# Attention inside a hybrid encoder: query pairs turned in a projection bank, two fillers moved, the keys' banks reordered, and the gates' running maxima turned at the seventh head

## The chip, the cores and the metric

One core of a Trainium2 chip runs the whole program. Its engines are TensorE (PE, with PEld for the weight loads that overlap it), VectorE (DVE), ScalarE (ACT), GpSimd (POOL) and SyncE (SP), which here issues nearly all DMA transfers. Each engine works through its own list of instructions in order; semaphores let it wait for the others. The metric is the time of one execution on the device in microseconds (us), given as the median of several executions.

## The reference

The program is one layer of a bidirectional encoder on two inputs of 512 tokens by 1024 channels: a half-step SwiGLU network, a mixing block, a second half-step SwiGLU network and a last normalisation. The change touches the mixing block alone:

```python
h = rms_norm(x, mix_norm)
proj = h @ w_in                      # queries, keys, values, memory q/k/v, 16 gate columns, output gates
aq = apply_rope(rms_norm(aq, q_norm), cos, sin)      # 8 query heads of 64
ak = apply_rope(rms_norm(ak, k_norm), cos, sin)      # 2 key/value heads
att = gqa_block_attention(aq, ak, av)                # softmax(q k / 8) v over all 512 tokens
mem = mlstm_bidirectional(mq, mk, mv, gate_pre, mlstm_gate_bias, o_pre, mlstm_head_norm)
merged = sigmoid(g_att) * (att @ w_up_att) + sigmoid(g_mlstm) * (mem @ w_up_mlstm)
x = x + merged @ w_out
```

The memory (`mlstm`) runs over the tokens in both directions with four heads. It needs, per direction and head, cumulative sums of the logarithms of the forget gates and running maxima over the tokens, so that its exponentials stay bounded. In the kernel these come from the 16 gate columns.

## The kernel before, in words

All matrix products are in float32 accuracy: each operand is split into a rounded high part and the remainder, and a product is made of three matmuls of the parts. So a result that is to be multiplied again goes through a split, one ACT instruction (L715, the high part) and one DVE instruction (L716, the remainder).

The mixing block, `mix`, is run twice, first for `s=0`, about 640 to 983 us, then for `s=1`, about 983 to 1403 us. In each pass:

- `tok_proj` (matmuls at L800) projects the keys, the values and the 16 gate columns for the four blocks of 128 tokens into four PSUM banks, and then the queries. The banks come from pools: `mm` (three banks, `MM`), `pss` (two, `PS`), `pst` (two, `PT`) and `pso` (one, `PO`).
- `gates` turns the gate columns into logarithms, sums them up with six small float32 products (L970), and makes running maxima along the tokens in a tile of 32 rows (L980 and L981). It sends the rows to DRAM (`ebuf`, L979). `gate_tops` later transposes the running maximum and the total maximum back (L988 and L989), and a DVE copy (L990) puts them into `st`. `mem_scales` (L1070 to L1081) derives the memory's scales from that with a dozen small DVE steps.
- `mem_rows` loads a head's row from `ebuf` into all partitions (L1061) and adds a mask to it (L1064). Its results lie in slots 0 to 3 of an eight-slot tile called `box`: head 0 takes slot 0 for the loaded row of the first direction, slot 1 for its masked copy, and slots 2 and 3 for the second direction.
- Attention goes head by head and, within a head, by four blocks. `score(h, b)` (L1091) makes the scores of 128 queries against 512 keys in a `pss` bank; DVE takes the row maximum (L1094), ACT the exponential with its sum (L1096), DVE the reciprocal (L1097), and ACT (L1099) or DVE (L1101) the scaling. `turn_keys(Ps, kb)` transposes the four query blocks' probabilities for one block of keys into a `pst` bank (L1107) and splits the result (L715 and L716). `values` multiplies it with the values into `pso` (L1118).
- Before heads 2, 4 and 6, `q_turn` transposes two query heads with four small matmuls (`pair_turn`, L900) and evacuates them with ACT and DVE (L1041 and L1042).
- Between these steps stand fillers: single matmuls of independent gate projections (L820, 512 columns each) that `among(n)` places n at a time. Their results are taken by ACT and DVE (L864 and L865) from an `mm` bank.

Attention's matmuls and the fillers are kept on PE in the order in which the code calls them. All other instructions, and the whole lists of ACT, DVE and SP, are ordered by a scheduler that runs when the kernel is built. The loop is:

Of the kernel before, what the change touches and what calls it, by code (L numbers as in the profile page):

```python
# [16 lines left out]
P = 128  # L17
# [9 lines left out]
def encoder(ctx, tc, I, outs):  # L27
    nc = tc.nc
# [13 lines left out]
    def nm(s):  # L42
        n_id[0] += 1
        return f"{s}_{n_id[0]}"
# [8 lines left out]
    boxes = {}  # L53
# [6 lines left out]
    def T2(dtype=F32, tag="t2"):  # L60
        if tag in ("eb", "ac"):
            i = boxes[tag]
            boxes[tag] += 1
            return boxes["tile"][:, i % 4 + (4 if tag == "ac" else 0), :]
        if tag == "R":
            return spool.tile([P, S], dtype, tag="R", bufs=2, name=nm("R"))
        n = {"t2": 11, "f2": 4}[tag]
        return tpool.tile([P, S], dtype, tag=tag, bufs=n, name=nm(tag))
# [47 lines left out]
    def PT():  # L116
        return pt.tile([P, S], F32, tag="t", name=nm("pst"))

    def f(ap):
        return ap.bitcast(F32)  # L120
# [7 lines left out]
    ones = cpool.tile([P, P], F32, name="ones")  # L128
# [157 lines left out]
    def load_w(view, key, park=True):  # L286


        if key in parked:
            d, shape = parked[key]  # L290
            w2 = wpool.tile(shape, F32R, tag="w8", bufs=4, name=nm("w"))
            for i in range(2):
                nc.sync.dma_start(f(w2[:, i]), d[:, i])
            return w2[:, 0], w2[:, 1]
        raw = fetch_w(view)
        with shifted(-WEIGHTS):
            hi, lo = split_w(raw, V_)
        if not park:
            return hi, lo
        shape = [P, 2] + list(raw.shape[1:])  # L300
        parked[key] = d, _ = dpool.tile(shape, F32, name=nm("wpark")), shape
        for i, t in enumerate((hi, lo)):
            nc.sync.dma_start(d[:, i], f(t))
        return hi, lo
# [424 lines left out]
    tabs = []  # L729
# [41 lines left out]
    def go(*units):  # L771
        for load, comp in units:
            held.append((comp, load()))
            while len(held) > ahead[0]:
                c, w = held.pop(0)
                c(w)
# [6 lines left out]
    def tok_proj(xh, xl, cols, kk, done, banks):  # L783

        N = sum(n for _, n in cols)
        p = []

        def load(k0):
            return load_w([win_v[:, k0:k0 + kk, c:c + n] for c, n in cols], ("in", cols[0], k0))

        def comp(k0, w):
            wh, wl = w
            if not p:
                p.extend(b() for b in banks)
            for kl in range(kk):
                k = k0 + kl
                for b in range(4):
                    bs = slice(b * P, (b + 1) * P)
                    for i, (a, w_) in enumerate(((xh, wh), (xh, wl), (xl, wh))):
                        nc.tensor.matmul(p[b][:, :N], a[:, k, bs], w_[:, kl, :],  # L800
                                         start=(k == 0 and i == 0), stop=(k == KD - 1 and i == 2))
            if k0 + kk == KD:
                done(p)

        return [(lambda k0=k0: load(k0), lambda w, k0=k0: comp(k0, w)) for k0 in range(0, KD, kk)]
# [29 lines left out]

    OUT = 3
    FILLER = 5,3
    FIRST = 9

    def mix(s, xh, xl, early=None, extra=None, after=None):  # L840

# [8 lines left out]
        def F2(dtype=F32):  # L850
            return T2(dtype, "f2")
# [42 lines left out]
            yield tt(v, v, cg.unsqueeze(2).to_broadcast([P, 4, 2, DA]), op=ALU.mult)  # L894
            yield tt(v, v, m, op=ALU.add)

        def pair_turn(o, keep):
            p = PT()
            for b in range(4):
                keep(nc.tensor.transpose(p[:, b * P:(b + 1) * P], o[:, b, :], ident))  # L900
            return p
# [17 lines left out]
        qraw, rq = mg[:, 4:8, :], []  # L919
# [18 lines left out]
        def gs(tag):  # L938
            t = small(32, tag)
            return t, t.rearrange("p (d b h) -> p d b h", d=2, b=4)  # L940
# [7 lines left out]
        def gates():  # L948
            Gb = Gt.rearrange("p (b c) -> p b c", b=4)
            V_.tensor_tensor(Gb, Gb, gbias.unsqueeze(1).to_broadcast([P, 4, 16]), op=ALU.add)  # L950
            Gv = Gt.rearrange("p (b d g h) -> p b d g h", b=4, d=2, g=2)

            Fs, Fv = gs("Fs")
            Is, Iv = gs("Is")
            for dst, g in ((Fv, 1), (Iv, 0)):
                G_.tensor_copy(dst[:, 0], Gv[:, :, 0, g, :])
                for b in range(4):
                    G_.tensor_copy(dst[:, 1, 3 - b], Gv[:, b, 1, g, :])
            fa, _ = gs("fa")
            V_.scalar_tensor_tensor(fa, Fs, -1.0, Fs, op0=ALU.mult, op1=ALU.min)  # L960
            nc.scalar.activation(fa, fa, AF.Exp)
            nc.scalar.activation(fa, fa, AF.Ln, bias=1.0)
            nc.scalar.activation(warm, fa[:, 0:1], AF.Exp)
            Lt, _ = gs("Lt")
            V_.scalar_tensor_tensor(Lt, Fs, 0.0, fa, op0=ALU.min, op1=ALU.subtract)
            p = PT()
            for d in range(2):
                rhs = Lt[:, d * 16:(d + 1) * 16]
                for j, lhs in enumerate((tabs[2][:, 2 * d, :], tabs[2][:, 2 * d + 1, :], ones)):
                    nc.tensor.matmul(p[:, j * 32 + d * 16:j * 32 + (d + 1) * 16], lhs, rhs, start=True, stop=True)  # L970
            V_.tensor_copy(cs, p[:, 0:96])
            et, ev = gs("fa")
            V_.tensor_tensor(et, Is, cs[:, 32:64], op=ALU.add)
            p = PT()
            nc.tensor.transpose(p[0:32, 0:P], et, ident)
            rows = F2()[0:32]
            er, run = rows[:, 0:P], rows[:, P:2 * P]
            V_.tensor_copy(er, p[0:32, 0:P])
            nc.sync.dma_start(ebuf.rearrange("d b h s -> (d b h) s"), er)  # L979
            V_.tensor_tensor_scan(run[:, ::-1], er[:, ::-1], er[:, ::-1], NEG, op0=ALU.max, op1=ALU.max)  # L980
            V_.tensor_tensor_scan(run[0:16], er[0:16], er[0:16], NEG, op0=ALU.max, op1=ALU.max)  # L981
            top = rows[:, 2 * P:2 * P + 1]
            V_.tensor_reduce(top, er, axis=AX.X, op=ALU.max)
            return run, top
# [50 lines left out]
        def q_rope(pr):  # L1035
            return rope_steps(qraw[:, :, pr * P:(pr + 1) * P], rq[0][:, :, 2 * pr:2 * pr + 2], tabs[0])

        def q_turn(pr, keep):
            p = pair_turn(qraw[:, :, pr * P:(pr + 1) * P], keep)
            for h, own, other in ((2 * pr, lower, upper), (2 * pr + 1, upper, lower)):  # L1040
                nc.scalar.activation(qT[own, h, :], p[own, :], AF.Copy)  # L1041
                V_.tensor_tensor(qT[other, h, :], p[own, :], f(qT[own, h, :]), op=ALU.subtract)  # L1042

        go(*tok_proj(xh, xl, [(512, 256), (2304, 16)], 2, kv_done, (PS, PS, MM, MM)))
        if early:
            early()
        go(*tok_proj(xh, xl, [(0, 512)], 2, q_done, (MM, PO, MM, MM)), mem_qk(0, 0), mem_qk(0, 1))
# [88 lines left out]
        def among(n):  # L1136
            for _ in range(n):
                if not between:
                    if not held:
                        return  # L1140
                    c, w = held.pop(0)
                    if queue:
                        load, c2 = queue.pop(0)
                        held.append((c2, load()))
                    between.extend(c.steps(w))
                between.pop(0)()
# [6 lines left out]
        for b in range(4):  # L1153
            Ps.append(score(0, b))
            next(rope, None)
            among(FIRST)
        last = None
        for h in range(HA):
            nxt = []
            for b in range(4):  # L1160
                if h in (0, 2, 4) and b == 2:
                    q_turn(h // 2 + 1, pin)
                if (h, b) == (0, 1):
                    gate_tops(*tops)
                if (h, b) in ((0, 3), (2, 3)):
                    rope = q_rope(h // 2 + 2)
                if h < 4:
                    next(rope, None)
                if h + 1 < HA:
                    nxt.append(score(h + 1, b))  # L1170
                among(FILLER[0])
                pp = turn_keys(Ps, b)
                among(FILLER[1])
                if last:
                    values(*last)
                last = h, b, pp
                if extra and b == 2 and h in (2, 3, 4):
                    extra[h - 2]()
            Ps = nxt
# [320 lines left out]
    def keep(k, eng=None):  # L1500
        pin(keep_x(0, k, banks[k], x0r[k], eng))
# [156 lines left out]
    def mid_parts(s):  # L1658
# [10 lines left out]
        return one, two, three  # L1669

    m0 = mix(0, *nhl[0], None, mid_parts(1), prep1)
    for _ in range(3):
        next(m0)
# [182 lines left out]
```

## Time and profile before

| | |
|---|---|
| time, median of 3 runs | 2051.71 us (2050.15 to 2051.81) |
| profiled execution, its own time | 2048.82 us |
| span of that execution | 2047.0 us |
| mean granted TensorE clock | 0.999 |
| PE busy | 2033.1 us (99%) |
| DVE busy | 1571.5 us (77%) |
| ACT busy | 909.0 us (44%) |
| POOL busy | 93.4 us (5%) |

The rows of the profile name an engine, a line, an operation, the tiles (result<-operands), the shape and a count. A bracket at the end of a timeline row gives the idle time of the engine before the instruction and what ended it. PE's matmuls are pipelined: a row's length runs into the next row's start. The time from one start to the next is what a matmul occupies.

### The profile page before, as it was taken

The numbers are of one execution on the slowest core, as the hardware profiler recorded it, in microseconds if no ns is written. First come the engines' busy times: TensorE is split into PE (matmuls) and PEld (weight loads), VectorE is DVE, ScalarE is ACT, GpSimd is POOL, SyncE is SP. The second block draws the span as 40 slices with busy tenths as digits, with TensorE's granted clock in tenths as the row PEclk, the third lists the DMA queues.
The fourth block names the chain that finished last, engine by engine and source line by source line (L and its number), as shares of the span: only waits on it lengthen the run. The fifth ranks groups of instructions, "written<-read, shape, count | busy, mean of one in ns | idle before, by whom it ended". The sixth has DMA issues, their size and how long they took to land.

```text
span 2047.0 us, 26767 instructions
## 1 busy us (share of the span) xinstructions
PE 2033.1 (99%) x9317; PEld 1679.9 (82%) x9317; DVE 1571.5 (77%) x2780; ACT 909.0 (44%) x1655; POOL 93.4 (5%) x116
## 2 busy tenths in 40 slices
PE   9999999999999999999999999999999999999998
PEld 7888888888888878888888888888888888888887
DVE  8888888886797888776567756366788988786797
ACT  7544444443234567563324554134544444442224
POOL 0000000001003000100120000001000000000001
PEclk9999999999999999999999999999999999999999
DMA  9656566799766853868564345667655655599753
GB/s 316 199 168 226 174 203 194 240 339 357 262 224 225 292 164 128 286 212 289 187 190 137 117 150 174 221 202 228 193 186 184 197 175 183 198 345 347 272 200 119
DMA packets 314727, 445.38 MB, mean 218 GB/s; under 512 B 19848, under 2 KB 189920, under 8 KB 313312
## 3 DMA queue, kind: packets, MB, share of 16 engines
q1 hardware_dynamic: 312512, 437.69, 63.8%
q0 software_dynamic: 1920, 5.72, 0.9%
q8 instruction: 73, 1.20, 0.2%
q14 instruction: 62, 0.51, 0.1%
q10 hardware_dynamic: 160, 0.27, 0.0%
HBM read 284.06 MB, written 159.55 MB: 217 GB/s over the span
## 4 chain that ended last, share of the span: by engine, by line
PE 95%; DVE 3%; ACT 1%; DMA 0%; issue 0%; SPq 0%; DVEq 0%; ACTq 0%
PE mm L833 16%; PE pst L374 12%; PE pso L374 12%; PE mm L374 11%; PE mm L632 8%; PE pss L374 6%; PE pst L632 4%; PE pss L632 4%; PE mm L820 4%; PE mm L800 4%; PE pso L632 3%; PE pso L1118 1%; PE pst L1107 1%; PE pss L1091 1%; PE pso L1287 1%; PE pss L1237 1%
## 5 line engine op out<-in xcount | busy, mean ns | idle before, releaser
L374 PE MATMUL pst<-xc,w 128*128 128x512 f32 x1056 | 253.7, 389 | 0.0
L374 PEld LDWEIGHTS pst<-xc,w 128*128 128x128 f32 x1056 | 198.3, 188 | 41.1
L374 PE MATMUL mm<-xc,w 128*128 128x512 f32 x972 | 229.4, 390 | 0.0
L374 PEld LDWEIGHTS mm<-xc,w 128*128 128x128 f32 x972 | 182.0, 188 | 37.7 <-ACT f L382 0.2
L632 PE MATMUL mm<-rt,w 128*128 128x512 f32 x765 | 178.7, 389 | 0.0
L833 PE MATMUL mm<-xh,w 128*128 128x512 f32 x560 | 176.9, 392 | 0.0
L632 PEld LDWEIGHTS mm<-rt,w 128*128 128x128 f32 x765 | 143.5, 188 | 29.7
L332 ACT ACTIVATE w<-t 128x512 fp32r<-128x512 f32 x176 | 106.6, 627 | 135.5 <-issue 63.1
L333 DVE TENSOR_TENSOR w<-t,w 128x512 fp32r<-128x512 f32 x176 | 117.8, 688 | 42.5 <-ACT w L332 41.0
L374 PE MATMUL pso<-xc,f 128*128 128x512 f32 x528 | 126.8, 389 | 0.0
L374 PE MATMUL pss<-xc,w 128*128 128x512 f32 x528 | 126.8, 389 | 0.0
L374 PE MATMUL pso<-xc,w 128*128 128x512 f32 x528 | 126.8, 389 | 0.0
L833 PEld LDWEIGHTS mm<-xh,w 128*128 128x128 f32 x560 | 104.9, 188 | 21.8
L374 PEld LDWEIGHTS pss<-xc,w 128*128 128x128 f32 x528 | 99.1, 188 | 20.6
L374 PEld LDWEIGHTS pso<-xc,w 128*128 128x128 f32 x528 | 99.1, 188 | 20.5
L374 PEld LDWEIGHTS pso<-xc,f 128*128 128x128 f32 x528 | 99.1, 188 | 20.6
L820 PE MATMUL mm<-xh,w 128*128 128x512 f32 x336 | 114.5, 401 | 0.0
L833 PE MATMUL mm<-xl,w 128*128 128x512 f32 x280 | 109.6, 391 | 0.0
L715 ACT ACTIVATE w<-wr 128x512 fp32r<-128x512 f32 x72 | 45.1, 632 | 136.7 <-PE pso L632 70.7
L278 ACT ACTIVATE w<-wr 128x1024 fp32r<-128x1024 f32 (+1 forms) x64 | 65.3, 1029 | 80.5 <-issue 23.7
L279 DVE TENSOR_TENSOR w<-wr,w 128x1024 fp32r<-128x1024 f32 (+1 forms) x64 | 79.8, 1248 | 27.7 <-ACT w L278 16.8
L715 ACT ACTIVATE w<-t 128x512 fp32r<-128x512 f32 x82 | 51.8, 632 | 107.6 <-PE pst L632 62.4
(440 smaller groups left out, 4067.0 us busy)
## 6 DMA issues: line engine op xcount, KB each, us to landing
rt<-rbuf SPq DMA_DIRECT2D x154, 512.0 KB, 5.7
wpark<-w SPq DMA_DIRECT2D x88, 512.0 KB, 3.5
w<-wpark SPq DMA_DIRECT2D x88, 512.0 KB, 4.5
wr<-in_ffn_w_gate_dram SPq DMA_DIRECT2D x62, 512.0 KB, 5.4
rbuf<-tab SPq DMA_DIRECT2D x102, 256.0 KB, 4.0
wr<-in_ffn_w_up_dram SPq DMA_DIRECT2D x44, 512.0 KB, 4.5
rbuf<-f SPq DMA_DIRECT2D x72, 256.0 KB, 4.0
wr<-in_w_in_dram SPq DMA_DIRECT2D x36, 512.0 KB, 5.6
```

The costliest lines, as they stand in the source:

```text
L278: pin(nc.scalar.activation(hi, raw, AF.Copy))
L279: pin(lo_eng.tensor_tensor(lo, raw, f(hi), op=ALU.subtract))
L332: pin(nc.scalar.activation(t[:, 0], src, AF.Copy))
L333: pin(V_.tensor_tensor(t[:, 1], src, f(t[:, 0]), op=ALU.subtract))
L374: nc.tensor.matmul(p, a[:, k, :], xt[:, b, k, :], start=(first and k == 0 and i == 0), stop=(k == HK_ - 1 and i == 2), skip_group_check=True)
L632: nc.tensor.matmul(p, u[:, a, d * P:(d + 1) * P], r[:, b, ts], start=(first and q == 0 and k == 0), stop=(q == len(us) - 1 and k == 2), sk ...
L715: nc.scalar.activation(hi, src, AF.Copy)
L800: nc.tensor.matmul(p[b][:, :N], a[:, k, bs], w_[:, kl, :], start=(k == 0 and i == 0), stop=(k == KD - 1 and i == 2))
L820: pin(nc.tensor.matmul(p[0], a[:, k, :], b, start=(k == 0 and i == 0), stop=(k == n - 1 and i == 2)))
L833: nc.tensor.matmul(p, a[:, k, :], b, start=(k == 0 and i == 0), stop=(k == n - 1 and i == 2))
L1091: pin(nc.tensor.matmul(p, qT[:, h, b * P:(b + 1) * P], kv[:, hk * 2 + j, :], start=(j == 0), stop=(j == 1)))
L1107: pin(nc.tensor.transpose(p[:, b * P:(b + 1) * P], Ps[b][:, kb * P:(kb + 1) * P], ident))
```

## The change

Five things change, all of them in `mix`.

1. `q_turn` of the pairs 1 to 3 transposes into an `mm` bank; pair 0 stays in a `pst` bank.
2. Of the fillers after the first four scores, the first score has two fewer behind it and the fourth two more (7, 9, 9, 11 for four times 9). In each head's first block, seven fillers stand before `turn_keys` and one behind it, where there were five and three.
3. `gate_tops` is called at block 1 of head 6, where it was called at block 1 of head 0. Its rows now lie in slot 0 of `box`, where they had a buffer of their own.
4. The two products with the matrix of ones, 16 columns each, become one of 32 columns.
5. In the second pass the four banks of the keys' projection come in the order `pss`, `mm`, `mm`, `pss`, where they were `pss`, `pss`, `mm`, `mm`.

```diff
     FILLER = 5,3
-    FIRST = 9
+    SOON = 7,1
+    FIRST = 7,9,9,11
...
-        def pair_turn(o, keep):
-            p = PT()
+        def pair_turn(o, keep, bank=PT):
+            p = bank()
...
-                for j, lhs in enumerate((tabs[2][:, 2 * d, :], tabs[2][:, 2 * d + 1, :], ones)):
-                    nc.tensor.matmul(p[:, j * 32 + d * 16:j * 32 + (d + 1) * 16], lhs, rhs, start=True, stop=True)
+                for j in range(2):
+                    nc.tensor.matmul(p[:, j * 32 + d * 16:j * 32 + (d + 1) * 16], tabs[2][:, 2 * d + j, :], rhs,
+                                     start=True, stop=True)
+            nc.tensor.matmul(p[:, 64:96], ones, Lt, start=True, stop=True)
...
-            rows = F2()[0:32]
+            rows = boxes["tile"][0:32, 0, :]
...
-            p = pair_turn(qraw[:, :, pr * P:(pr + 1) * P], keep)
+            p = pair_turn(qraw[:, :, pr * P:(pr + 1) * P], keep, MM if pr else PT)
...
-        go(*tok_proj(xh, xl, [(512, 256), (2304, 16)], 2, kv_done, (PS, PS, MM, MM)))
+        go(*tok_proj(xh, xl, [(512, 256), (2304, 16)], 2, kv_done, (PS, MM, MM, PS) if s else (PS, PS, MM, MM)))
...
-            among(FIRST)
+            among(FIRST[b])
...
-                if (h, b) == (0, 1):
+                if (h, b) == (6, 1):
                     gate_tops(*tops)
...
-                among(FILLER[0])
+                n0, n1_ = FILLER if b else SOON
+                among(n0)
                 pp = turn_keys(Ps, b)
-                among(FILLER[1])
+                among(n1_)
```

Line numbers of the changed kernel are larger by 1 from `pair_turn` on, by 3 behind the small products and by 4 in the end of the loop. The order of the instructions, as the scheduler now makes it, shows three places.

On PE, in the first pass at head 4, block 2: the query pair's transposes (`mg` holds the queries), the score of the next head, five fillers, and the turn of the probabilities. Before:

```order
L1118 MATMUL pso_6594<-t_622_6555,kv_5275 128x512
L900 MATMUL pst_6597<-ident,mg_5279 128x128 x4
L1091 MATMUL pss_6606<-kv_5275,qT_5278 128x512 x2
L820 MATMUL mm_6547<-xh_4894,w_6429 128x512
L820 MATMUL mm_6547<-xl_4895,w_6429 128x512
L820 MATMUL mm_6547<-xh_4894,w_6429 128x512 x2
L820 MATMUL mm_6547<-xl_4895,w_6429 128x512
L1107 MATMUL pst_6620<-ident,t_583_6384 128x128 [waits DVE_49,PE_49]
```

Now:

```order
L1121 MATMUL pso_6588<-t_620_6551,kv_5275 128x512
L901 MATMUL mm_6591<-ident,mg_5279 128x128 x4
L1094 MATMUL pss_6600<-kv_5275,qT_5278 128x512 x2
L820 MATMUL mm_6541<-xh_4894,w_6423 128x512
L820 MATMUL mm_6541<-xl_4895,w_6423 128x512
L820 MATMUL mm_6541<-xh_4894,w_6423 128x512 x2
L820 MATMUL mm_6541<-xl_4895,w_6423 128x512
L1110 MATMUL pst_6614<-ident,t_581_6378 128x128
```

The order is the same; the query pair has moved to an `mm` bank, and the first transpose of the probabilities has no wait any more.

On SP, in the first pass around head 6: stores of split weights to DRAM (`wpark`), loads of raw weights (`wr`), and the load of the first head's row (`box<-ebuf`). Before, with the first head's two loads standing 32 rows earlier:

```order
L271 DMA wr_7146<-in_w_up_att_dram 128x4x256 [waits DMAHW7_49]
L303 DMA wpark_7051<-w_7048 128x1024 [waits DMAHW0_49,Activation_49]
L303 DMA wpark_7051<-w_7048 128x1024 [waits DMAHW1_49,DVE_49]
L271 DMA wr_7276<-in_w_in_dram 128x8x128 [waits DMAHW2_49]
L1061 DMA box_5274<-ebuf_5281 128x4x128 [waits DMAHW3_49,Activation_49]
```

Now:

```order
L271 DMA wr_7144<-in_w_up_att_dram 128x4x256 [waits DMAHW6_49]
L1064 DMA box_5274<-ebuf_5281 128x4x128 [waits DMAHW7_49,PE_49]
L303 DMA wpark_7049<-w_7046 128x1024 [waits DMAHW0_49,Activation_49]
L303 DMA wpark_7049<-w_7046 128x1024 [waits DMAHW1_49,DVE_49]
L271 DMA wr_7274<-in_w_in_dram 128x8x128 [waits DMAHW2_49]
L1064 DMA box_5274<-ebuf_5281 128x4x128 [waits DMAHW3_49,Activation_49]
```

One of the two loads of head 0 has moved here from the beginning of the attention, and it waits for PE.

On DVE, in the first pass at head 6, now, from the copy of the turned maxima, which follows the remainder split of turn (6,0), to the remainder split of turn (6,1):

```order
L993 COPY st_5282<-pst_6822 128x64 [waits PE_49]
L1133 TENSOR_TENSOR f_653_6697<-pso_6727,f_681_6817 64x512 [waits Activation_49]
L1097 TENSOR_REDUCE asm_6829<-pss_6826 128x1 [waits PE_49]
L865 TENSOR_TENSOR mg_5279<-mm_6745,R_5146 128x512 [waits PE_49]
L1076 TENSOR_TENSOR st_5282<-st_5282 128x2x4 [waits DVE_49]
L1078 TENSOR_TENSOR st_5282<-st_5282,cs_5280 128x32
L1097 TENSOR_REDUCE asm_6856<-pss_6853 128x1 [waits PE_49]
L716 TENSOR_TENSOR att_5856<-f_653_6697,att_5856 128x512 [waits Activation_49]
L1100 RECIPROCAL asm_6829<-asm_6829 128x1 [waits Activation_49]
L1075 TENSOR_TENSOR st_5282<-st_5282,cs_5280 128x2x4 [waits DVE_49]
L1067 TENSOR_TENSOR box_5274<-box_5274,tab_4214 128x512 [waits DMAHW7_49]
L716 TENSOR_TENSOR t_688_6847<-pst_6841,t_687_6846 128x512 [waits Activation_49]
```

The copy of the maxima, small steps of `mem_scales` and the mask add of head 0 (L1064 before, L1067 now) stand here now; before, they stood among the first blocks of head 0, and the mask add ahead of the scaling of block 3.

## The prediction

> **What bounds the kernel now.** I read the busy times of the page first, then the shares of the chain of waits, then the busy time by stretches, and last the timeline of TensorE (PE) around each hole.
>
> ```profile
> PE 2033.1 (99%) x9317; PEld 1679.9 (82%) x9317; DVE 1571.5 (77%) x2780; ACT 909.0 (44%) x1655; POOL 93.4 (5%) x116
> PE 95%; DVE 3%; ACT 1%; DMA 0%; issue 0%; SPq 0%; DVEq 0%; ACTq 0%
> 640.00:983.00 343.00, 340.64 (x1647) 279.77 (x1645) 269.28 (x570) 196.56 (x382) 29.77 (x33) 1.00 0.70 232
> 983.00:1403.00 420.00, 418.95 (x1995) 346.73 (x1996) 246.33 (x549) 167.60 (x351) 28.91 (x38) 1.00 0.54 172
> 700.00:720.00 20.00, 19.45 (x88) 15.66 (x87) 19.69 (x39) 10.70 (x20) 0.00 (x0) 1.00 0.81 258
> ```
>
> PE is busy 99% of the span and is 95% of the chain, at the full granted clock (1.00). So time can be saved only by removing PE work or PE's holes. The stretch rows give length, then busy time of PE, PEld, DVE, ACT, POOL, clock, DMA share and GB/s. Between 640 and 983 us (the first mixing pass) PE has holes of 343.00 - 340.64 = 2.36 us, between 983 and 1403 (the second) 1.05 us: 3.41 us in all. These are the holes:
>
> ```profile
> 753.06 0.39 PE L820 MATMUL mm<-xl,w 128*128 128x512 f32 x1
> 753.29 0.39 PE L820 MATMUL mm<-xh,w 128*128 128x512 f32 x1
> 753.97 0.63 PE L1107 MATMUL pst<-ident,t 128*128 128x128 f32 x4 [0.29 <-DVE qT L1042]
> 717.56 0.33 PE L1107 MATMUL pst<-ident,t 128*128 128x128 f32 x1 [0.55 <-DVE t L1101]
> 758.43 0.33 PE L1107 MATMUL pst<-ident,t 128*128 128x128 f32 x1 [0.72 <-ACT t L1099]
> 778.55 0.63 PE L1107 MATMUL pst<-ident,t 128*128 128x128 f32 x4 [0.31 <-DVE t L716]
> 983.28 0.52 PE L800 MATMUL pss<-w,xh 128*128 128x272 f32 x2 [0.77 <-DVE t L1218]
> 1098.46 0.63 PE L1107 MATMUL pst<-ident,t 128*128 128x128 f32 x4 [0.71 <-DVE t L716]
> ```
>
> The bracket is the idle time and who ended it. The first two rows show a matmul of 0.39 us followed by the next after 0.23: 0.16 us of its length lies under the next one. A hole therefore costs its bracket plus 0.16 (753.97 - 753.29 - 0.23 = 0.45 = 0.29 + 0.16). The six cost 0.45, 0.71, 0.88, 0.47, 0.93 and 0.87 us, together 4.3. That is the most that removing waits can give.
>
> **Part 1, query pairs in a projection bank: -1.8 us.** The holes at 753.97, 778.55 and 1098.46 are transposes of the probabilities (L1107) that wait for one of the two `pst` banks, because a query pair's four transposes hold the other until VectorE (DVE) has evacuated it. All three follow a query turn in the same block. In the order now, these transposes wait for nothing at head 4, and the query turn into `mm` waits for nothing at any of the three pairs. The three `mm` banks have slack, since a filler's bank lives for many matmuls. Removed: 0.45 + 0.47 + 0.87 = 1.79. Nothing is added; a filler that found its bank still held would wait for two evacuations of 0.6 to 0.7 each, which I put at nothing, as the query turn takes a bank and releases it within one block. Bounds: 1.3 to 1.8.
>
> **Part 2, two fillers moved: -1.2 us.** At 717.56 and 758.43 the fourth transpose waits for the scaled probabilities of block 3, whose score was issued last. The score of (0,3) now has two fillers fewer ahead of it and the turn two more behind: the turn comes 2 x 0.23 = 0.45 later, and the same 0.45 at each head's first block.
>
> ```profile
> 711.77 0.68 DVE L1064 TENSOR_TENSOR box<-box,tab 128x512 f32<-128x512 f32 x1
> 717.02 0.48 DVE L1101 TENSOR_SCALAR t<-t,asm 128x512 f32<-128x512 f32 x1
> 757.04 0.73 ACT t L1096 x2
> 757.76 0.62 ACT t L1099
> ```
>
> At 717 the DVE is full (19.69 of 20 us above), so a later need alone gives 0.45 of the 0.71. But the mask add of L1064 (0.6 us: 0.68 less what the next instruction overlaps) leaves this stretch, against a rope step of 0.33 to 0.6 that moves up: DVE ends the scaling 0.27 earlier. 0.45 + 0.27 = 0.72 covers the hole: -0.71. At 758 the scale stood behind two exponentials on ScalarE (ACT). Here I take the 0.45 of the move alone, of 0.88, since PE also arrives earlier by what parts 1 and 2 save. Bounds: nothing (the chain on DVE and ACT moves with PE) to 1.59.
>
> **Part 3, banks for the keys' projection: -0.75 us.**
>
> ```profile
> 983.76 0.41 PE L800 MATMUL mm<-w,xh 128*128 128x272 f32 x2
> 984.14 0.41 PE L800 MATMUL mm<-w,xh 128*128 128x272 f32 x2
> 982.62 0.61 DVE t L1218
> ```
>
> The second `pss` bank is read by DVE until 983.23. One block of three matmuls takes 984.14 - 983.76 = 0.38; two such blocks on `mm` now stand ahead of it, so 0.76 of the 0.93 is filled and about 0.18 stays. Bounds: 0.7 to 0.93.
>
> **Part 4, one matmul instead of two: -0.2 us.**
>
> ```profile
> 686.23 1.25 PE pst L970 x12
> ```
>
> Twelve PE instructions (six fp32 products, two passes each) take 1.25 us, 0.104 each. One product fewer saves 0.21 in each pass. In the first pass PE then only arrives earlier at the full DVE of 700 to 720 and I count nothing; in the second it counts. Bounds: 0.2 to 0.42.
>
> **Part 5, the running maxima are turned at head 6: +0.6 us.** PE's two small transposes only move. What is new is that their rows now occupy the box slot into which the first head's gates are loaded, so that load (L1061) cannot start before PE has turned them. Before it was issued at 695; nobody waited.
>
> ```profile
> L1061 SPq DMA_DIRECT2D box<-ebuf x16: 370/434/2921, 695.2 to 1248.0; - x16
> DMA to landing us min/median/max: 3.4/5.1/7.1
> 794.58 0.46 SPq L271 DMA_DIRECT2D wr<-in_w_up_att_dram  x1
> 804.75 1.96 SPq L303 DMA_DIRECT2D wpark<-w  x2
> 797.83 0.60 PE L1107 MATMUL pst<-ident,t 128*128 128x128 f32 x4
> 798.18 0.70 PE L820 MATMUL mm<-xh,w 128*128 128x512 f32 x2
> 798.72 0.39 PE L820 MATMUL mm<-xl,w 128*128 128x512 f32 x1
> 799.41 0.62 PE L1091 MATMUL pss<-kv,qT 128*128 128x512 f32 x2
> 802.16 0.62 PE L1091 MATMUL pss<-kv,qT 128*128 128x512 f32 x2
> 802.80 0.69 DVE L716 TENSOR_TENSOR t<-pst,t 128x512 fp32r<-128x512 f32 x1
> 799.00:806.00 7.00, 7.00 (x38) 5.59 (x37) 6.45 (x12) 6.10 (x13) 0.00 (x0) 1.00 0.08 29
> ```
>
> In the first pass the transposes stand before the score at 799.41, so the load is issued at about 799.8. SyncE's queue (SP) has nothing between its issues at 794.58 and 804.75, so the load is not late there and nothing behind it is. It lands at 803.2, 804.9 or 806.9 by the least, median and longest landing. On DVE the mask add stands ahead of the remainder split (L716) of turn (6,1), the row of 802.80. In DVE's new order there stand ahead of the mask the row maximum of the score at 802.16, which cannot start before that score is there at about 803.0, the split of the attention tile and some steps of under 0.1: 803.0 + 0.6 + 0.6 + 0.2, so it reaches the mask at about 804.4, adds 0.6 and ends the split 0.7 later, at 805.7. PE gets to the product that needs it after 21 wide matmuls of 0.23 and two turns of 0.43 (798.72 - 797.83, less the two matmuls in it): 799.6 + 5.7 = 805.3. So 0.4 is lost even if the load is in time; with the median landing 0.9, with the longest 2.9. The DMA engines are busy 8% there, so I take a landing below the median: 0.4. The Trainium skill's page "SBUF — State Buffer", section "The DMA setup-cost knee", has a transfer at 2 us plus its bytes at 436 GB/s, an estimate of 2.6 us for these 256 KB. No load here landed in under 3.4; by the page the third rival below would be impossible, and the 0.4 would stay.
>
> ```profile
> 1171.65 0.62 PE L1091 MATMUL pss<-kv,qT 128*128 128x512 f32 x2
> 1173.77 0.62 ACT L715 ACTIVATE att<-f 128x512 fp32r<-128x512 f32 x1
> 1175.40 0.69 DVE L716 TENSOR_TENSOR t<-pst,t 128x512 fp32r<-128x512 f32 x1 [0.21 <-ACT t L715]
> 1177.58 0.62 PE L1118 MATMUL pso<-t,kv 128*128 128x512 f32 x2
> ```
>
> In the second pass the load is issued at about 1172.0 and lands at 1175.4, 1177.1 or 1179.1. DVE is at the mask at about 1175.0 (its row maximum and a 0.6 us split of the attention tile, which ACT hands over at about 1174.4, stand ahead) and waits. The split (now at 1175.40) ends 1.3 after landing: 1176.7, 1178.4 or 1180.4, and PE needs it for the second product at 1177.8, 0.2 later with the transposes: 0, 0.4 or 2.4 us lost. Together 0.4 to 5.3, with medians 1.3; I take 0.6. Queued behind the mask on DVE are also a row maximum and a scale of head 7, which are needed only some microseconds later.
>
> **The sum.** -1.79 - 0.71 - 0.45 - 0.75 - 0.21 + 0.6 = -3.3 us. Against the profiled execution (2048.82 us, span 2047.0) that is 2045.5; that execution lies 2.9 below the median of the runs shown, 2051.71, on which I forecast 2048.4.
>
> **The rivals.** (1) Every hole goes and the load lands in time: -1.8 - 1.59 - 0.93 - 0.42 = -4.7, 2047.0 us. For it: the stretch behind 720 loses DVE work (the maxima's copy, the small steps and a mask), so the chain at 758 may be on time. Against it: the 0.4 of DVE work at head 6. (2) The softmax chain moves with PE, and the two moved fillers buy nothing, so that the change doesn't do what its order says. -3.3 + 1.16 = -2.1, 2049.6. For it: DVE and ACT, not PE, set 700 to 760. Against it: at 717 the DVE list itself is shorter by the mask. (3) The wait goes from a bank to the mask on DVE: the load lands after 7 us in both passes, DVE stands still in front of the split, and PE loses 5.3: -3.9 + 5.3 = +1.4, 2053.1, slower. It decides from a loss of 3.9, a landing of about 6.4 us in both passes. For it: the longest landing seen is 7.1, and PE passes the point of need 5.5 to 6 us after the issue. Against it: the idle DMA engines, and a median of 5.1.
>
> **How the numbers follow.** Forecast 0.52 (its own range 2047.6 to 2049.4), rival 1 0.25, rival 2 0.15, rival 3 0.08. Less than 0.2%, 4.1 us, cannot be told from no change here. Faster by more needs rival 1 or the forecast's far end: 0.26. Slower by more than 4.1 needs losses beyond the longest landing: 0.05. The rest, 0.69, is within. The range goes from rival 1 with 0.7 more for the spread of the runs (2050.15 to 2051.81), 2046.3, to near rival 3, 2052.4.
>
> **What would show it.** After: no hole at L1107 for a `pst` bank behind a query turn; the hole at 983 cut to 0.2 or gone; ten instead of twelve instructions at the gates; PE's holes in the two passes down from 3.4 us to about 1. A new hole at a product (L1118 now) near 805 and 1178, ended by L716, shows part 5; one over 2 us there shows rival 3. Holes at 717 and 758 of the old size show rival 2. Holes in places where none was before, at a filler's `mm` bank above all, would make the forecast wrong.

## The result and the profile after

The changed kernel takes 2046.17 us (median of 15 runs, 2044.83 to 2047.98). The kernel before, in the runs made beside them and the three shown earlier, takes 2050.34 us (15 runs, 2048.41 to 2051.81). The ratio is 0.998, 95% interval 0.9973 to 0.9988: a gain of about 4.2 us, between 2.5 and 5.5. The profiled execution of the changed kernel took 2045.07 us, span 2043.3, against 2048.82 and 2047.0 before.

The forecast was 2048.4 us in a range of 2046.3 to 2052.4, a gain of 3.3. The time lies 0.13 us under the range. What follows is on why the gain is near the forecast while the time is 2.2 us below it.

The busy times of the page of the changed kernel, and its busy time by the two mixing passes (length, then PE, PEld, DVE, ACT, POOL, clock, DMA share, GB/s):

```profile
PE 2032.2 (99%) x9313; PEld 1679.4 (82%) x9313; DVE 1571.8 (77%) x2780; ACT 908.9 (44%) x1655; POOL 94.4 (5%) x116
640.00:983.00 343.00, 342.35 (x1663) 281.82 (x1661) 272.58 (x570) 196.98 (x382) 31.00 (x33) 1.00 0.70 234
983.00:1403.00 420.00, 419.94 (x1992) 347.29 (x1991) 246.01 (x551) 169.22 (x354) 28.81 (x38) 1.00 0.54 173
```

PE's holes in the two passes went from 2.36 and 1.05 us to 0.65 and 0.06. PE's timeline in the changed kernel at the places of the six old holes, and the new ones (start, length, instruction, idle time and releaser):

```profile
716.18 0.70 PE L1110 MATMUL pst<-ident,t 128*128 128x128 f32 x4
752.05 0.60 PE L1110 MATMUL pst<-ident,t 128*128 128x128 f32 x4
755.76 0.83 PE L1110 MATMUL pst<-ident,t 128*128 128x128 f32 x4
775.42 0.60 PE L1110 MATMUL pst<-ident,t 128*128 128x128 f32 x4
980.98 0.28 PE L800 MATMUL mm<-w,xl 128*128 128x272 f32 x1
981.27 0.52 PE L800 MATMUL pss<-w,xh 128*128 128x272 f32 x2
1094.12 0.60 PE L1110 MATMUL pst<-ident,t 128*128 128x128 f32 x4
732.90 0.40 PE L820 MATMUL mm<-xh,w 128*128 128x512 f32 x1
733.39 0.51 PE L1121 MATMUL pso<-t,kv 128*128 128x512 f32 x1
857.43 0.93 PE L1241 MATMUL pss<-qk 128*128 128x512 f32 x3 [0.55 <-DVE t L1257]
```

The three transposes behind query turns stand without a bracket: those holes are gone. Of the one at 717 about 0.1 is left (four transposes in 0.70 instead of 0.60), of the one at 758 about 0.2 (0.83; 0.17 of it in one step), of the one at the keys' projection 0.18 (981.27 - 980.98, less the 0.11 that such a matmul occupies), and a step of 0.49 at 732.90, 0.26 too long, is new; it ends when DVE has read the `pso` bank (its L1133 ends at 733.34). So is the last row new: 0.71 us before a product of the memory heads near 857. By steps from one start to the next, against the usual step of a matmul of that shape, the holes of over 0.12 us between 640 and 1403 us come to about 4.8 before and 1.8 now.

At the gates, ten instructions in 1.04 us (the chain of waits of the changed kernel) stand for twelve in 1.25:

```profile
685.68 0.80 PE pst L971 x8
686.48 0.24 PE pst L973 x2
```

Executions of one program differ ahead of the mixing passes: the first key product of the first pass begins between 645.49 and 647.83 us in the eighteen traces of this case. The clean comparison begins with the first key product of the first mixing pass and ends with PE's last group of matmuls. Before, first and last row of that stretch in PE's timeline:

```profile
646.63 0.41 PE L800 MATMUL pss<-w,xh 128*128 128x272 f32 x2
...
2039.07 1.24 PE L648 MATMUL mm<-w,rt 128*128 128x256 f32 x9
```

And now:

```profile
646.06 0.41 PE L800 MATMUL pss<-w,xh 128*128 128x272 f32 x2
...
2035.35 1.24 PE L648 MATMUL mm<-w,rt 128*128 128x256 f32 x9
```

That is 1392.44 before and 1389.29 now: 3.15 us less. The rest of the 3.7 between the spans is the start. To PE's very last matmul, 0.96 later in both, it is 1393.40 and 1390.25; this is the length that the experiments are compared by.

### The profile page after: what moved, and what is told of

Its sections match the earlier page's. It is cut to its first block, busy times and chain, and to the rows that moved or that the text cites. A ratio compares the mean times of both kernels' runs of the same rounds, so it can differ in the third digit from the quotient of the medians.

```text
span 2043.3 us, 26748 instructions
## 1 busy us (share of the span) xinstructions
PE 2032.2 (99%) x9313; PEld 1679.4 (82%) x9313; DVE 1571.8 (77%) x2780; ACT 908.9 (44%) x1655; POOL 94.4 (5%) x116
## 4 chain that ended last, share of the span: by engine, by line
PE 98%; DMA 1%; DVE 1%; ACT 0%; issue 0%; SPq 0%; DVEq 0%; ACTq 0%
PE mm L833 16%; PE pso L374 12%; PE pst L374 12%; PE mm L374 11%; PE mm L632 8%; PE pss L374 6%; PE mm L820 6%; PE pss L632 4%; PE pst L632 4%; PE mm L800 4%; PE pso L632 3%; PE pso L1121 1%; PE pss L1094 1%; PE pst L1110 1%; PE pso L1291 1%; PE pso L800 1%
```

## The experiments

All of them start from the changed kernel, if nothing else is said. Each has its timed ratio to the kernel before, and its length as above against 1390.25. The intervals of nearly all the ratios overlap, so it is the lengths that tell the versions apart, most of them from one trace each.

**One part undone at a time.** Query pairs in `pst` again:

```diff
-            p = pair_turn(qraw[:, :, pr * P:(pr + 1) * P], keep, MM if pr else PT)
+            p = pair_turn(qraw[:, :, pr * P:(pr + 1) * P], keep)
```

> The changed kernel with one part undone: the query pairs 1 to 3 are turned in a `pst` bank again. Theory A (each part's gain is its own holes, and they add up): the holes at the turn of the probabilities behind a query turn return, about 0.45 near 750, 0.47 near 775 and 0.87 near 1094, so PE's holes in the two passes grow from 1.9 to about 3.7 us and the span from 2043.3 to about 2045.1. Rival (with the work of the running maxima gone from the start of the attention, DVE evacuates the banks in time anyway): the holes near 750 and 1094 stay away, and the span grows by 0.5 or less.

Measured: length 1391.82, +1.57; ratio 0.9989 (0.998 to 0.9999). PE's timeline has the three holes back, of the old sizes:

```profile
751.99 0.63 PE L1110 MATMUL pst<-ident,t 128*128 128x128 f32 x4 [0.31 <-DVE qT L1045]
775.59 0.63 PE L1110 MATMUL pst<-ident,t 128*128 128x128 f32 x4 [0.31 <-DVE t L716]
1095.19 0.63 PE L1110 MATMUL pst<-ident,t 128*128 128x128 f32 x4 [0.71 <-DVE t L716]
```

Theory A holds. The rival falls: less work on DVE does not free the bank in time.

The fillers where they were:

```diff
-    SOON = 7,1
-    FIRST = 7,9,9,11
+    SOON = 5,3
+    FIRST = 9,9,9,9
```

> The changed kernel with the fillers where they were (9, 9, 9, 9 and 5, 3). Theory A (the moved fillers hide the softmax): a hole of 0.3 to 0.7 returns near 716 and one of 0.4 to 0.9 near 757, the span grows by 0.7 to 1.4 us. Rival B (the work of the running maxima that left the start of the attention made the softmax early): both holes stay under 0.3, the span grows by 0.4 at most.

Measured: length 1391.54, +1.29; ratio 0.9987 (0.9978 to 0.9997). Two holes are back in PE's timeline, 0.56 and 1.28 us with the 0.16 that the brackets leave out:

```profile
717.55 0.33 PE L1110 MATMUL pst<-ident,t 128*128 128x128 f32 x1 [0.40 <-DVE t L1104]
757.82 0.33 PE L1110 MATMUL pst<-ident,t 128*128 128x128 f32 x1 [1.12 <-ACT t L1102]
```

The first is in the expected range, the second above it: the hole that was 0.89 before has grown to 1.28. Counted from the first key product, PE reaches it 1.4 us earlier than before, and the scaled probabilities come 1.0 earlier. The small step at 733 is gone, and the hole near 857 is 0.93. It is the fillers that hide most of the softmax.

The maxima turned at head 0, with rows of their own:

```diff
-            rows = boxes["tile"][0:32, 0, :]
+            rows = F2()[0:32]
...
-                if (h, b) == (6, 1):
+                if (h, b) == (0, 1):
```

> The changed kernel with the running maxima turned at head 0 again, their rows in a buffer of their own. Theory A (moving them neither cost nor gained, since the load landed ahead of DVE's mask add): no hole of over 0.3 us near 716 and 757, span within 0.4 of 2043.3. Rival B (their leaving is what emptied DVE): holes of together 0.6 to 1.5 us near 716 and 757 return. The new hole of 0.7 near 856: if it comes from PE having gained time against GpSimd's mask adds, which wait for a transfer, it stays or changes by how much PE has gained; if it comes from the maxima's move, it goes.

Measured: length 1390.22, -0.03; ratio 0.9978 (0.9968 to 0.9987). In steps of PE, 0.29 came back near 716 and 0.16 stayed near 756; the 0.71 near 857 is not there. So moving the maxima was worth nothing in sum, but not because it did nothing: of rival B there is about 0.3 us near 716, where DVE has its mask add again (at 710.94), and the move has a part in the hole near 857, which by the expectation's last sentence speaks for it as a cause. That hole needs its own look, below.

The keys' banks in their old order:

```diff
-        ... kv_done, (PS, MM, MM, PS) if s else (PS, PS, MM, MM)))
+        ... kv_done, (PS, PS, MM, MM)))
```

> The changed kernel with the keys' banks of the second pass in their old order. Theory A: the hole near 981 is 0.9 us again in place of 0.18, span about 2044.0. Rival (the split tile in that bank is late for another reason, GpSimd's part of the splits, and any gain ahead just grows the hole): the hole is larger than 0.94.

Measured: length 1391.09, +0.84; ratio 0.9983 (0.9974 to 0.9992). The step is 0.94 too long, as before. Its row:

```profile
982.86 0.52 PE L800 MATMUL pss<-w,xh 128*128 128x272 f32 x2 [0.77 <-DVE t L1222]
```

The two products with ones apart again:

```diff
-                for j in range(2):
-                    nc.tensor.matmul(..., tabs[2][:, 2 * d + j, :], rhs, start=True, stop=True)
-            nc.tensor.matmul(p[:, 64:96], ones, Lt, start=True, stop=True)
+                for j, lhs in enumerate((tabs[2][:, 2 * d, :], tabs[2][:, 2 * d + 1, :], ones)):
+                    nc.tensor.matmul(..., lhs, rhs, start=True, stop=True)
```

> The changed kernel with the two products with ones apart again. Theory A: twelve instructions at the gates take 1.25 us in place of about 1.04, in each pass; nothing else changes, PE's holes stay, span +0.2 to +0.4. Rival: the first pass's 0.2 us is eaten at the full DVE of 700 to 720, so that only 0.2 shows.

Measured: length 1390.62, +0.37; ratio 0.9978 (0.9969 to 0.9987). Holes as in the changed kernel. The gain is near twice the 0.2 of one pass, so both passes save it.

So the parts are worth 1.57 + 1.29 + 0.84 + 0.37 - 0.03 = 4.04 us taken away one by one, and 3.15 together. The difference, 0.9, is of the size of the new hole near 857 with the small step at 733. Where one part is undone these change too (no step at 733 with the fillers back, no hole near 857 with the maxima back), so the single figures are not worths that add up.

**The load at head 6.** The rows in a buffer of their own, so that the first head's load is early, and the maxima turned at head 6:

```diff
-            rows = boxes["tile"][0:32, 0, :]
+            rows = F2()[0:32]
```

> The changed kernel with the rows of the maxima in a buffer of their own, so that the first head's load is early again, while the maxima are still turned at head 6. Theory A (at head 6 neither the load nor the mask add was late): no change there; DVE gets the mask add of 0.6 us back in the full stretch of 700 to 720, and a hole of 0.2 to 0.5 us returns near 716. Rival (the mask's place does not matter): span within 0.2 us of 2043.3.

Measured: length 1390.63, +0.38; ratio 0.9973 (0.9963 to 0.9983). A step of 0.28 too long is back, ending at 717.94, as theory A has it: DVE's mask add is in the full stretch again, at 712.12. The hole near 857 is 0.89, and one of 0.23 came at 891. At head 6 nothing changed, because nothing was lost there. The timeline of the changed kernel's SP, DVE and PE there, first pass:

```profile
796.61 0.37 SPq L1064 DMA_DIRECT2D box<-ebuf  x1
800.91 0.68 DVE L1067 TENSOR_TENSOR box<-box,tab 128x512 f32<-128x512 f32 x1
801.51 0.68 DVE L716 TENSOR_TENSOR t<-pst,t 128x512 fp32r<-128x512 f32 x1
802.56 0.40 PE L1121 MATMUL pso<-t,kv 128*128 128x512 f32 x1
```

The load landed 3.8 us after its issue, at 800.4, DVE reached the mask at 800.9 without a wait and ended the split at 802.2, and PE came to the product at 802.56.

**The hole near 857.** The timeline there, in the changed kernel: GpSimd adds two masks, and DVE's splits of that time are long.

```profile
852.71 3.01 POOL L1067 TENSOR_TENSOR box<-box,tab 128x512 f32<-128x512 f32 x2 [13.68 <-DMA box<-ebuf]
853.69 0.87 DVE L716 TENSOR_TENSOR qk<-f,qk 128x512 fp32r<-128x512 f32 x1
854.83 1.98 DVE L279 TENSOR_TENSOR w<-wr,w 128x1024 fp32r<-128x1024 f32 x1
```

Before, the same two took 0.69 and 1.22 (GpSimd's timeline, then DVE's):

```profile
852.96 1.29 POOL L1064 TENSOR_TENSOR box<-box,tab 128x512 f32<-128x512 f32 x1 [12.90 <-DMA box<-ebuf]
854.65 1.30 POOL L1064 TENSOR_TENSOR box<-box,tab 128x512 f32<-128x512 f32 x1 [0.41 <-DMA box<-ebuf]
856.61 0.69 DVE L716 TENSOR_TENSOR qk<-f,qk 128x512 fp32r<-128x512 f32 x1
857.55 1.22 DVE L279 TENSOR_TENSOR w<-wr,w 128x1024 fp32r<-128x1024 f32 x1
```

And with the maxima at head 0, where the hole is not there:

```profile
850.98 2.58 POOL L1067 TENSOR_TENSOR box<-box,tab 128x512 f32<-128x512 f32 x2 [13.22 <-DMA box<-ebuf]
854.30 0.69 DVE L716 TENSOR_TENSOR qk<-f,qk 128x512 fp32r<-128x512 f32 x1
855.25 1.22 DVE L279 TENSOR_TENSOR w<-wr,w 128x1024 fp32r<-128x1024 f32 x1
```

Two ways to test it: the mask adds of heads 1 to 3 on DVE, or on GpSimd twice.

```diff
-            (V_ if s or not h else G_).tensor_tensor(em3, eb3, ..., op=ALU.add)
+            V_.tensor_tensor(em3, eb3, ..., op=ALU.add)
```

> The changed kernel with the memory heads' mask adds of the first pass (heads 1 to 3) on DVE in place of GpSimd. Theory A (the hole near 856 is DVE's two-input instructions held up while GpSimd adds masks: the remainder split of a weight took 1.98 us there and takes 1.22 elsewhere): the long instruction is back at 1.2 us, the hole goes, and PE gains up to 0.7 us, less what six more instructions of 0.69 us cost DVE. Rival (DVE is late at 856 by its list): the hole stays at 0.5 or grows.

Measured: length 1390.13, -0.12; ratio 0.9978 (0.997 to 0.9987). The splits are back at 0.68 and 1.22, as theory A says, but the hole only went from 0.71 to 0.59 and stands earlier, ahead of the product at 856.02: now DVE itself waits for the transfer, ahead of what PE needs (DVE's timeline).

```profile
852.65 0.69 DVE L1067 TENSOR_TENSOR box<-box,tab 128x512 f32<-128x512 f32 x1 [3.07 <-DMA box<-ebuf]
854.67 0.68 DVE L716 TENSOR_TENSOR qk<-f,qk 128x512 fp32r<-128x512 f32 x1
855.89 1.22 DVE L279 TENSOR_TENSOR w<-wr,w 128x1024 fp32r<-128x1024 f32 x1
```

```diff
-            (V_ if s or not h else G_).tensor_tensor(em3, eb3, ..., op=ALU.add)
+            for _ in range(1 if s or not h else 2):
+                (V_ if s or not h else G_).tensor_tensor(em3, eb3, ..., op=ALU.add)
```

> The changed kernel with each mask add of GpSimd (memory heads 1 to 3 of the first pass) done twice, the second time with the same result. Theory A (GpSimd and DVE block each other on two-input instructions): near 856 DVE's two-input instructions are longer still or more of them are long, and the hole grows from 0.7 to over 1.2 us. Rival: GpSimd is off the path and the hole is DVE's list: 0.7 as before.

Measured: length 1392.03, +1.78; ratio 0.9979 (0.997 to 0.9988). Neither theory had this: the transfer landed so late that the adds began behind the two splits, which took 0.69 and 1.22, and the hole near 857 was gone. Instead small DVE steps on the denominators, 0.17 us elsewhere, took over a microsecond under the doubled adds, and PE lost 2.03 us at 862.65 (timelines of GpSimd, DVE and PE):

```profile
854.16 7.18 POOL L1068 TENSOR_TENSOR box<-box,tab 128x512 f32<-128x512 f32 x4 [13.88 <-DMA box<-ebuf]
857.91 1.17 DVE L1262 SCALAR_TENSOR_TENSOR dn<-dn 128x8 f32<-128x8 f32 x1
860.13 1.24 DVE L1263 TENSOR_TENSOR dn<-dn,st 128x8 f32<-128x8 f32 x1
862.65 1.02 PE L1284 MATMUL pst<-ident,t 128*128 128x128 f32 x6 [1.87 <-DVE t L1270]
```

So the two engines do block each other, and the place of the hole follows the place of the adds. Two versions turn the maxima at other blocks, which changes when that load is issued:

```diff
-                if (h, b) == (6, 1):
+                if (h, b) == (4, 1):
```

> The changed kernel with the running maxima turned at head 4, block 1 in place of head 6. The list of SyncE then keeps its old order of loads near 840 us. Theory A (the hole near 856 comes from GpSimd's mask adds falling on DVE's two-input splits): if the adds start 1 us or more earlier than in the changed kernel (652.7 there, counted from the first mixing pass 206.7), the splits take 0.7 and 1.2 us and the hole goes, 0.5 to 0.7 us gained; DVE's mask add for head 0 then falls in head 4 and 5 and may cost 0 to 0.5 there. Rival: the hole stays at over 0.5 with the splits at their normal length.

The 652.7 of this expectation is 852.7 in the trace, 206.7 behind the first key product. Measured: length 1390.89, +0.64; ratio 0.998 (0.9971 to 0.9988). The adds ran from 851.53 to 854.13, the splits began at 855.26, took 0.69 and 1.22, and the hole near 857 was gone. A hole of 0.84 came ahead of 836.35, where ACT began a weight's rounding late for a reason that the profile does not show, and one of 0.19 at 891.

```diff
-                if (h, b) == (6, 1):
+                if (h, b) == (6, 2):
```

> The changed kernel with the running maxima turned one block later, at head 6, block 2. SyncE keeps its old order near 840 us as well. Theory A as for the version at head 4: the hole near 856 goes if GpSimd's adds start 1 us or more earlier against DVE's splits, and stays with a long split if not. At head 6 and 7 the load has one block less until DVE needs its result, so a hole of up to 0.5 us may come near 806.

> The version with the maxima turned at head 6, block 2, once more. Theory A (GpSimd's mask adds end before DVE's two-input splits begin, by the order of SyncE's loads): no hole over 0.3 near 856 again, length from the first key product to PE's last matmul 1389.6 within 0.3. Rival (it was the luck of one landing): the hole of 0.7 is back, length 1390.2.

Measured in two traces: lengths 1389.59 and 1390.29; ratios 0.9974 (0.9965 to 0.9984) and 0.9979 (0.9969 to 0.9989). The first trace has no hole near 857, the second 0.69; both have one of 0.2 near 890 and none near 806. GpSimd's adds and DVE's splits, first trace and then second:

```profile
851.09 2.55 POOL L1067 TENSOR_TENSOR box<-box,tab 128x512 f32<-128x512 f32 x2 [12.56 <-DMA box<-ebuf]
853.59 0.69 DVE L716 TENSOR_TENSOR qk<-f,qk 128x512 fp32r<-128x512 f32 x1
854.54 1.22 DVE L279 TENSOR_TENSOR w<-wr,w 128x1024 fp32r<-128x1024 f32 x1
```

```profile
852.08 2.56 POOL L1067 TENSOR_TENSOR box<-box,tab 128x512 f32<-128x512 f32 x2 [13.59 <-DMA box<-ebuf]
853.56 1.62 DVE L716 TENSOR_TENSOR qk<-f,qk 128x512 fp32r<-128x512 f32 x1
855.45 1.22 DVE L279 TENSOR_TENSOR w<-wr,w 128x1024 fp32r<-128x1024 f32 x1
```

The rival of the second trace holds: the order of the loads does not remove the hole, one landing 1 us earlier did. It is the same in all traces with the adds on GpSimd: in the eight where the second add ended before the first split began or within 0.05 of it (the five of before and the one with the maxima at head 0 among them), both splits were of normal length; in the eight where an add was still running when a split began, one or both were long; where the adds began only behind both splits (the doubled ones), both were normal. This version is not shown to beat the changed kernel.

**Second traces.** Both kernels once more, without an edit, and the kernel before three times more.

> The changed kernel once more, for a second trace and a narrower interval. Theory A: the same length is 1390.2 us within 0.3, so the change gains 3.1 to 3.2 us where it acts; the timed ratio comes out at 0.9979 to 0.9985. Rival (the gain is the 4.2 us of the medians, and the trace of before was a good one): ratio at or under 0.998 and a length of 1393.8 or more for before. The hole near 856 is 0.4 to 0.9, since it hangs on when a transfer lands.

> The kernel before once more, for a second trace. Theory A (the executions of one program differ in the first 50 us, where PE waits for the inputs, and hardly behind): from the first key product of the first mixing pass to PE's last matmul 1393.4 us, as in the first trace, within 0.3; the six holes have the sizes of the first trace within 0.1; only the start of the first mixing pass differs, between 645.4 and 647.9 us. Rival (the holes themselves scatter from one execution to the next): the length differs by over 0.5.

Measured: the changed kernel 1390.21, with the same holes (0.77 near 857), ratio 0.9976 (0.9967 to 0.9985). The kernel before 1394.09, not 1393.40; the ratio of the two copies is 0.9997 (0.9987 to 1.0006). So the rival has it: the first trace of before was a good one. The six holes came back within 0.01 us; the 0.69 stands in a seventh place, at 1229, where the step is 0.82 too long; the first trace of before had it at 0.13, and the forecast passed over it.

> The kernel before, a third trace. In its first trace a hole near 1229 cost 0.13 us, in its second 0.82, because DVE's mask add waited for a load that landed 5.8 us after its issue. Theory C (the kernel before often loses 0.7 there and the changed kernel does not): 0.6 or more in most of the three traces of this call, length from the first key product to PE's last matmul 1394.0. Rival (the second trace was the exception): 0.13, length 1393.4.

> The kernel before, a fourth trace, with the expectations of the third: 0.6 or more near 1229 by theory C, 0.13 by the rival.

> The kernel before, a fifth trace, with the expectations of the third: 0.6 or more near 1229 by theory C, 0.13 by the rival.

Measured: 1.24, 0.13 and 1.18 us at that place, lengths 1394.67, 1393.52 and 1394.57. The third trace of before:

```profile
1229.10 0.69 DVE L1064 TENSOR_TENSOR box<-box,tab 128x512 f32<-128x512 f32 x1 [1.02 <-DMA box<-ebuf]
1230.67 0.96 PE L1237 MATMUL pss<-qk,qk 128*128 128x512 f32 x3 [1.08 <-DVE t L1253]
```

DVE's mask add of a later memory head waits for its load (the first of a pair; it landed 5.8 to 6.2 us after its issue in the three traces with the hole, 4.8 and 4.9 in the two without), the score's product behind it in DVE's list is late, and PE waits. In three of five traces of before this costs 0.7 to 1.1 us more than in the first, 0.57 on the mean. In all the traces of the changed kernel and its versions the step there is 0.12 to 0.14 too long and DVE does not wait; the load landed after 4.8 to 5.1 in all thirteen. Theory C holds, though no run shows why the load is never late there now.

## Why the prediction missed, point by point

**The level.** The step that failed first is the last one of the sum, the level on which the gain was set: the forecast put it under 2051.71, the median of three runs, and over fifteen the kernel before takes 2050.34. That is 1.37 of the 2.23 us by which the forecast missed, and it alone carries the time out of the range: its low end stood 0.7 under the farthest case to allow for the spread of the runs, though the profiled execution, 2048.82, lay 2.9 under that median and was already a warning. In the traces the scatter sits ahead of the first key product, which the five of before reach at 646.07 to 647.03 us (they are 1.2 us apart by 46 us), and in two holes: from the first key product, executions of one program agree within 0.2 us but for the holes at 1229 and 857.

**The sum.** Forecast -3.3; by the first traces of both -3.15. By all traces of before (mean length 1394.05) and the two of the changed kernel -3.8; timed -4.2 (2.5 to 5.5) and in the second comparison -4.9 (3.1 to 6.8). The other 0.86 of the miss is the gain. The term that the sum lacked is the hole at 1229: I took the one profiled execution for all executions, and a wait that hangs on a landing is not of one size. Adding its mean of 0.57 gives -3.9. What of the timed gain is left over, 0.3 to 1, is within the intervals. That -3.15 by the first traces lies so near -3.3 is in part luck: the 0.6 of part 5 was not lost, and two waits that were not in the sum, 0.71 near 857 and 0.26 at 733, were. By its conditions rival 1 came nearest: the load landed in time in both passes, and the six holes went but for about 0.5 us.

**Part 1**, -1.79: right, 1.57 by undoing it, the three holes each with its size.

**Part 2**, -1.16: right in sum, 1.29. The hole at 717 went but for 0.1, though not quite by the 0.45 + 0.27 told: with the mask add back in that stretch 0.28 returns, with the fillers back 0.56. At 758, 0.72 of 0.89 went, where 0.45 was taken. The bound of zero, rival 2, falls.

**Part 3**, -0.75: right, 0.76 from the step itself (0.94 to 0.18), 0.84 by undoing it.

**Part 4**, -0.21: too small, 0.37. What failed here is that the first pass was put at nothing. PE's 0.2 there was not lost at the full DVE, since the hole at 717 had room left.

**Part 5**, +0.6: wrong. The walk along DVE's list gave the split at 6.1 us behind the transposes, and it came at 5.7 (802.2 less 796.5); PE was said to need it 5.7 behind them and did after 6.05. Each end was off by 0.4 to the bad side, and the loads landed after 3.8 and 3.3 us, near the shortest of 3.4 in the trace of before. Undoing the move gives 0.03, but that is a balance of the 0.3 near 716 and the hole near 857. Rival 3, the slower one, would have needed 6.4 twice. The Trainium skill's page "SBUF — State Buffer", section "The DMA setup-cost knee", would have it at an estimate of 2.6 us; 3.3 and more are measured in the changed kernel.

**What nobody had**: the 0.7 near 857. Counted from the first key product, DVE's split of `qk` came there 2.3 us earlier than before (853.69 instead of 856.61, of which 0.57 is the start), while the first of GpSimd's two adds, which wait for transfers, came 0.3 later and the second 0.1 earlier. So they met. The maxima's move has a part in it: in the one trace with them at head 0, DVE's split comes 0.6 later than in the changed kernel, the two loads are issued 1.3 and 2.1 us earlier, and the second add ends 0.7 before the split. The landing has a part too, as the two traces of head 6, block 2 show. How much of the 0.7 goes to each is not separated. The forecast said that holes in new places, a filler's bank above all, would make it wrong; this one stands at a memory head, and by that sign it was. It ate a fifth of what the parts gain one by one.

## What to carry to other kernels

When all the gain is PE's holes, add up the holes first: the four parts that fill holes or remove work came within 0.3 us each, and the one that was put down as a cost was off by 0.6. But a hole that ends with a transfer has to be looked at in several traces, and a time that is near the spread of the runs is to be forecast as a difference, with the level from as many runs as there are. An engine that gets ahead of another which is paced by transfers can run into it: list what the other engines do at the times that the work moves to.

## What the runs showed of the hardware

GpSimd and DVE hold each other up. A DVE instruction with two operands in SBUF (the memory on the chip that holds the tiles; matmuls write to PSUM, another) that begins while GpSimd's add runs takes about as long as the rest of that add and its own time: 1.98 us instead of 1.22, 0.80 to 1.82 instead of 0.69, and a step on eight columns 1.17 instead of 0.17. DVE instructions that read one operand from PSUM, as the scores' products do, kept their time (0.69 at 853.08, in the midst of the adds). The Trainium skill's page "SBUF — State Buffer", section "SBUF: two separate sides", says that the two share a port pair as an exclusive lock which a DVE instruction with two such inputs takes for its whole length against a GpSimd instruction that reads there, and that the other is blocked; these traces agree. GpSimd pays too: two adds took 3.01 us, with DVE's split ending between them, where they took 2.55 to 2.60 in other traces.

Transfers of 256 KB of one kind landed after 3.3 to 7.2 us within one execution, and the same transfer at the same place (the first of the pair at 1222) after 4.8 to 6.2 us in five executions of one program. Why it landed after 4.8 to 5.1 in all thirteen traces of the changed kernel and its versions is not shown.
